# 128 more bytes ahead of the left-hand rooms of a decoder-layer kernel

## The chip, the cores and the metric

One core of one Trainium2 chip runs one launch of the kernel. The metric is the device time of that launch in microseconds (us), as the median of several runs. Lower is better.

## What is computed

One decoder layer over 1024 positions of width 1024, in float32 (each weight below is one layer's):

```python
h = rms_norm(x, ln_pre_mix)
proj = h @ w_in                      # pooling inputs (256), q, k, v (768 each)
q, k = rope(q, pos), rope(k, pos)    # 12 heads of 64
pool_out = multi_scale_pool(u_pool, w_pool, pool_scale)
attn_out = dilated_attention(q, k, v)        # three (window, dilation) settings, merged
mix = concatenate([pool_out, attn_out]) @ w_out
x = x + rms_norm(mix, ln_post_mix)
h = rms_norm(x, ln_pre_ffn)
f = (silu(h @ w_gate) * (h @ w_up)) @ w_down   # inner width 2816
x = x + rms_norm(f, ln_post_ffn)
```

## The kernel before

**Arithmetic.** Every large product is made in three passes: each operand is split into a high and a low half (ScalarE copies the high one, VectorE or GpSimd subtracts it for the low one), and TensorE adds up high x high, high x low and low x high (`PASSES`, line 167). So a product of one 128 x 128 weight block with 512 positions is three matmuls, each with its own weight load. In a matmul's name in the profile, `ps_o<-tT,fw 128*128 128x512` is: result in bank `o`, moving operand from a room `tT`, stationary operand (weights) from a room `fw`, 128 x 128 weights, 512 moving columns. A name that is in one place only, `ps_t<-fw`, has both operands in rooms of that name.

**Stages.** They follow one another on TensorE, with some overlap. To about 100 us: the first query and key projections (`first`, line 223), the value and pooling projections. To about 440 us: attention (`scores`, `merge`, `weigh`, `values`, lines 512 to 701) with projections of later heads filled in between (`proj_half`, line 412; `Fill`, line 389), so that runs of 512-column matmuls are cut into pieces of a few. To about 521 us: the output projection (`out_proj`, line 902), the norms (`chain`, line 1024) and the first gate and up blocks. To about 947 us: the gate and up products as seven block products in place of eight (`seven`, line 1178), 24 matmuls of 512 columns to a product, with the sums of weight blocks for the next stage beside them. To the end: the down projection, also in seven block products (`down`, line 1442), then the last norm and the stores.

**Order.** A list of steps with due times, written out by hand (`put`, `emit`, the numbers in `PRM`), sets the order of the matmuls; the matmuls are kept in program order (line 116). Loads and stores go out on SyncE's queue.

**Rooms.** SBUF is filled from two sides. On the left, from low addresses up, lie the pools `const`, `wpool`, `small`, and above them first `con1` and `att`, later, in the same place, `ffnl`. On the right, from high addresses down, lie `xg`, then `qkp`, later, in the same place, `mid`. The lines that matter:

```python
32   LEAD = {"const": 8, "con1": 8, "ffnl": 8}
...
121  const = ctx.enter_context(tc.tile_pool(name="const", bufs=1))
122  wpool = ctx.enter_context(tc.tile_pool(name="wpool", bufs=1))
...
169  half = const.tile([P, 1 + LEAD["const"]], F32, name="half")[:, :1]
...
188  xgp = ctx.enter_context(tc.tile_pool(name="xg", bufs=1, side="right"))
...
1061 r3 = ffnl.tile([P, T + LEAD["ffnl"]], F32, name="r3")[:, :T]
...
1273 for a, bb in PASSES:
1274     mm(banks[tag, i], lhs[:, i, a, c * P:(c + 1) * P], moving(b, bb, c),
```

`half` is the first tile of the first left-hand pool. It holds one number per partition, -0.5, the exponent of the reciprocal square root (line 184); `LEAD["const"]` adds eight numbers behind it that nothing reads. All later left-hand tiles start above it, at multiples of 32 bytes. A tile's start, in bytes of its partition and modulo 256, in the allocation of this kernel:

| side, pool | tiles, by their names in the profile | start modulo 256 |
|---|---|---|
| left, `wpool` | `whl` (split weights; operands of the block products), `wraw` | 0 |
| left, `att` | `pp`, `ptr`, `v`, `mix`, `dhl`, `wp`, `xraw` | 128 |
| left, `ffnl` | `b` (the normed features, split; later operands), `rw`, `op`, `q` | 0 |
| right, `qkp` | `k`, `qh`, `ql`, `vs` | 128 |
| right, `mid` | `fw` (operands; a feature block), `p`, `sq`, `rb` | 128 |
| right, `xg` | `x`, `m`, `z`, `tT` (sums of feature blocks), `op`, `xk`, `vlast`, `y` | 128 |

A block of weights within a room starts at a multiple of 512 bytes from the room's start, and a 512-column moving operand at a multiple of 1024, so each matmul's operands start at their room's place modulo 256. (The exceptions are matmuls of under 512 columns with strided keys.)

Of the kernel before, what the change touches and what calls it, by code (L numbers as in the profile page):

```python
# [28 lines left out]

LEAD = {"const": 8, "con1": 8, "ffnl": 8}

PRM = {'sqe': (0, 0, 0, 0, 1, 1, 0, 1),
        'sqa': (1, 0, 0, 1, 0, 0, 0, 1),
# [75 lines left out]
def hybrid_block(ctx: ExitStack, tc: tile.TileContext, xT, w_in, w_v, w_pin, w_pool, w_out, w_gate, w_up, w_down,  # L111
# [56 lines left out]

    half = const.tile([P, 1 + LEAD["const"]], F32, name="half")[:, :1]
    nc.vector.memset(half, -0.5)  # L170
# [26 lines left out]

    g1s = con1.tile([P, NK + LEAD["con1"]], F32, name="g1s")[:, :NK]
    nc.sync.dma_start(g1s, g1)
# [860 lines left out]
    ffnl = ctx.enter_context(tc.tile_pool(name="ffnl", bufs=1))  # L1060
    r3 = ffnl.tile([P, T + LEAD["ffnl"]], F32, name="r3")[:, :T]
    B = {}
# [504 lines left out]
```

## Time and profile before

| | us |
|---|---|
| median of 3 runs (1175.99 to 1178.06) | 1177.0 |
| the profiled execution's own time | 1176.04 |
| its span, first to last instruction | 1174.3 |
| TensorE busy (matmuls) | 1140.2 |
| VectorE / GpSimd / ScalarE busy | 792.1 / 602.0 / 543.3 |

The profile lists groups of equal instructions as `line engine operation out<-in shape xcount | busy us, mean ns of one`. Matmuls are pipelined: a mean of 390 ns is from one matmul's start to its end, and the next starts about 230 ns behind it. So the pace is read from starts, or from a group's busy time over its count, and not from the mean. PE is TensorE's matmul stream, PEld its weight loads, DVE VectorE, ACT ScalarE, POOL GpSimd, SP SyncE. A window row gives busy time and instructions per engine, then the granted TensorE clock, the share of the 16 DMA engines and GB/s.

### The profile page before, as it was taken

The page shows a single profiled execution, that of the slowest core. Times are in us where ns is not written, and L with a number is a line of the kernel's source. Part 1 is how long each engine was busy: PE and PEld are TensorE (multiplying, and loading weights), DVE is VectorE, ACT ScalarE, POOL GpSimd, SP SyncE. Part 2 cuts the span into 40 slices and gives each one's busy share as a digit, 9 for nine tenths or more (in the row PEclk, how much of TensorE's full clock was granted, in tenths as well). Part 3 has the DMA queues.
Part 4 walks back from the last instruction along what each step waited for, and adds up shares of the span by engine and source line. Part 5 has one row for each costly group of instructions (what it writes and reads, how often), then busy time and mean ns, then how long its engine had stood idle before and what let it go on. Part 6 is the DMA issues. An engine that isn't in the chain of part 4 may idle for free.

```text
span 1174.3 us, 17248 instructions
## 1 busy us (share of the span) xinstructions
PE 1140.2 (97%) x6134; PEld 980.7 (84%) x6134; DVE 792.1 (67%) x1477; ACT 543.3 (46%) x1033; POOL 602.0 (51%) x541
## 2 busy tenths in 40 slices
PE   8999999999998999999999999999999999999996
PEld 6998898999888888878888888888888888888896
DVE  7766878786887674869676655756465475454685
ACT  7356666666566574746432232223232435343430
POOL 0111646464565413250486656777665978566521
PEclk9999999999899999999999999999999999999998
DMA  7315151514124745722234545444535859666542
GB/s 269 99 62 180 37 180 37 180 55 162 54 83 157 264 166 187 275 73 99 75 141 143 192 158 187 181 164 160 204 127 187 284 196 376 229 203 190 191 143 72
DMA packets 85365, 188.51 MB, mean 161 GB/s; under 512 B 8736, under 2 KB 24352, under 8 KB 83872
## 3 DMA queue, kind: packets, MB, share of 16 engines
q1 hardware_dynamic: 84704, 186.90, 45.7%
q8 instruction: 48, 0.79, 0.3%
q10 hardware_dynamic: 576, 0.52, 0.1%
q14 instruction: 37, 0.30, 0.1%
HBM read 134.44 MB, written 52.95 MB: 160 GB/s over the span
## 4 chain that ended last, share of the span: by engine, by line
PE 82%; DVE 7%; ACT 4%; DMA 3%; issue 2%; POOL 2%; SPq 0%; ACTq 0%; POOLq 0%; DVEq 0%
PE ps_pj L116 28%; PE ps_o L116 22%; PE ps_s L116 21%; PE ps_t L116 9%; PE ps_t L119 2%; ACT pp L559 1%; DMA mixd<-mix 1%; DMA b<-in_w_out_dram 1%; DVE k L348 1%; DMA xraw<-in_xT_dram 1%; DVE whl L159 1%; DVE ptr L656 1%; DMA m<-mixd 1%; DVE sq L1005 0%; POOL whl L159 0%
## 5 line engine op out<-in xcount | busy, mean ns | idle before, releaser
L116 PE MATMUL ps_pj<-x,whl 128*128 128x512 f32 x480 | 145.4, 417 | 0.0
L1221 POOL TENSOR_TENSOR fw<-rw,fw 128x512 fp32r<-128x512 f32 x74 | 100.5, 1383 | 65.2 <-ACT fw L1219 65.2
L611 POOL TENSOR_SCALAR pp<-pp,wv 128x256 f32<-128x256 f32 (+1 forms) x156 | 72.0, 481 | 104.1 <-DVE wv L595 51.4
L116 PE MATMUL ps_o<-tT,fw 128*128 128x512 f32 x504 | 117.7, 389 | 0.0
L159 POOL TENSOR_TENSOR whl<-wraw,whl 128x512 fp32r<-128x512 f32 x50 | 66.7, 1355 | 90.9 <-ACT whl L155 61.0
L116 PEld LDWEIGHTS ps_o<-tT,fw 128*128 128x128 f32 x504 | 94.6, 188 | 19.9
L559 ACT ACTIVATE pp<-pp,sx 128x128 f32<-128x128 f32 (+1 forms) x192 | 89.3, 468 | 29.8 <-DVE sx L556 29.3
L116 PEld LDWEIGHTS ps_pj<-x,whl 128*128 128x128 f32 x480 | 87.0, 194 | 10.3 <-POOL whl L159 0.4
L1221 POOL TENSOR_TENSOR whl<-rw,whl 128x512 fp32r<-128x512 f32 x42 | 60.3, 1459 | 57.7 <-ACT whl L1219 57.7
L1219 ACT ACTIVATE fw<-rw 128x1024 fp32r<-128x1024 f32 x37 | 38.5, 1056 | 99.3 <-DVE rw L1187 34.3
L116 PE MATMUL ps_pj<-whl,x 128*128 128x256 f32 x528 | 80.6, 293 | 0.0
L1363 POOL TENSOR_TENSOR op<-rw,op 128x512 fp32r<-128x512 f32 x38 | 59.9, 1577 | 36.9 <-ACT op L1362 34.4
L656 DVE TENSOR_TENSOR ptr<-ps_t,ptr 128x512 fp32r<-128x512 f32 (+1 forms) x84 | 56.2, 669 | 25.0 <-ACT ptr L655 24.4
L116 PEld LDWEIGHTS ps_pj<-whl,x 128*128 128x128 f32 x528 | 70.8, 196 | 0.5 <-DVE whl L159 0.2
L1362 ACT ACTIVATE op<-rw 128x1024 fp32r<-128x1024 f32 x38 | 40.2, 1060 | 64.2 <-PE ps_t L116 27.0
L325 POOL TENSOR_TENSOR rsw<-rsw,sinr 128x512 f32<-128x512 f32 x20 | 26.2, 1310 | 84.5 <-DVE rsw L323 84.5
L655 ACT ACTIVATE ptr<-ps_t 128x512 fp32r<-128x512 f32 (+1 forms) x84 | 48.5, 577 | 40.9 <-PE ps_t L119 39.7
L116 PE MATMUL ps_o<-ptr,v 128*128 128x128 f32 (+1 forms) x472 | 58.8, 258 | 5.3 <-DVE ptr L656 5.3
L116 PE MATMUL ps_pj<-b,fw 128*128 128x512 f32 x264 | 63.3, 395 | 0.0
L116 PEld LDWEIGHTS ps_o<-ptr,v 128*128 128x128 f32 x472 | 52.4, 164 | 9.5 <-DVE ptr L656 6.4
L116 PEld LDWEIGHTS ps_pj<-b,fw 128*128 128x128 f32 x264 | 49.6, 188 | 11.9
L116 PE MATMUL ps_s<-k,qh 128*128 128x128 f32 (+1 forms) x192 | 53.6, 291 | 0.3 <-DVE sx L556 0.2
(302 smaller groups left out, 2917.2 us busy)
## 6 DMA issues: line engine op xcount, KB each, us to landing
rw<-bd SPq DMA_DIRECT2D x77, 256.0 KB, 4.9
v<-vd SPq DMA_DIRECT2D x22, 512.0 KB, 4.5
rw<-wsd SPq DMA_DIRECT2D x44, 256.0 KB, 4.0
rw<-in_w_gate_dram SPq DMA_DIRECT2D x20, 512.0 KB, 3.6
rw<-in_w_up_dram SPq DMA_DIRECT2D x20, 512.0 KB, 4.6
bd<-p SPq DMA_DIRECT2D x33, 256.0 KB, 2.5
rw<-in_w_down_dram SPq DMA_DIRECT2D x33, 256.0 KB, 4.6
fw<-in_w_down_dram SPq DMA_DIRECT2D x16, 512.0 KB, 4.0
```

The source lines that it names most:

```text
L116: return tc.keep_in_program_order(nc.tensor.matmul(*a, **k))
L119: return tc.keep_in_program_order(nc.tensor.transpose(dst, src, by))
L159: eng.tensor_tensor(dst[:, 1, at:at + w], src[:, at:at + w], dst[:, 0, at:at + w].bitcast(F32), ALU.subtract)
L325: eng[0].tensor_tensor(s, s, sinr[:, sl], ALU.mult)
L559: nc.scalar.activation(pt[:, j, lo:], pt[:, j, lo:], AF.Exp, bias=sx[:, 0, side, j, hd, 0:1], scale=-1.0, accum_out=sx[:, 0, side, j, hd, ...
L611: nc.gpsimd.tensor_scalar(pv, pv, un.wv[:, side, j, hd:hd + 1], 1.0, op0=ALU.mult, op1=ALU.mult)
L655: nc.scalar.activation(ptr[:, 0, :w], t[:, :w], AF.Copy)
L656: nc.vector.tensor_tensor(ptr[:, 1, :w], t[:, :w], ptr[:, 0, :w].bitcast(F32), ALU.subtract)
L1219: nc.scalar.activation(w[n][:, :, 0], raw[n], AF.Copy)
L1221: low[0] = nc.gpsimd.tensor_tensor(w[n][:, i, 1], raw[n][:, i], w[n][:, i, 0].bitcast(F32), ALU.subtract)
L1362: nc.scalar.activation(w[:, :, 0], raw, AF.Copy)
L1363: nc.gpsimd.tensor_tensor(w[:, 0, 1], raw[:, 0], w[:, 0, 0].bitcast(F32), ALU.subtract)
```

## The change

```diff
-LEAD = {"const": 8, "con1": 8, "ffnl": 8}
+LEAD = {"const": 40, "con1": 8, "ffnl": 8}
```

`half` grows from 36 to 164 bytes per partition. All left-hand tiles behind it move up by 128 bytes; the right-hand ones stay. Modulo 256, `wpool` and `ffnl` go from 0 to 128 and `att` from 128 to 0, while `qkp`, `mid` and `xg` stay at 128. Between the end of `att` and the start of `qkp` 256 bytes were free, so both still fit. No instruction is added, removed or moved; operands on the same side keep their distance.

## The prediction

> **What bounds the kernel now.** I read the busy times first, then the chain of waits, then the engines by stage, then the matmul groups by form in the stage that carries most.
>
> ```profile
> PE 1140.2 (97%) x6134; PEld 980.7 (84%) x6134; DVE 792.1 (67%) x1477; ACT 543.3 (46%) x1033; POOL 602.0 (51%) x541
> ...
> PE 82%; DVE 7%; ACT 4%; DMA 3%; issue 2%; POOL 2%; SPq 0%; ACTq 0%; POOLq 0%; DVEq 0%
> ```
>
> TensorE is busy nearly throughout and is 82% of the chain that ended last. The stages differ, though:
>
> ```profile
> 100.00:440.00 340.00, 325.21 (x2158) 297.47 (x2158) 266.02 (x779) 219.53 (x582) 166.98 (x215) 0.98 0.38 129
> 440.00:521.00 81.00, 78.00 (x391) 64.12 (x390) 51.85 (x64) 48.17 (x80) 27.89 (x25) 0.98 0.55 195
> 521.00:947.00 426.00, 425.91 (x1861) 348.08 (x1860) 271.38 (x323) 140.33 (x184) 272.24 (x199) 1.00 0.45 162
> 947.00:1174.30 227.30, 216.21 (x1096) 184.58 (x1094) 134.90 (x174) 83.43 (x91) 119.75 (x79) 0.98 0.59 200
> ```
>
> Columns: stretch, its length, busy time of PE, PEld, DVE, ACT, POOL, clock, DMA share, GB/s. From 521 to 947 us, the gate and up products, TensorE has no gap at all (425.91 of 426.00), at full clock; whatever a matmul costs there is paid in the end time, one for one. In attention (100 to 440) TensorE shares the path with others. So the question is whether the place of the operands changes what a matmul costs. In this stage the same matmul, 128 x 128 weights and 512 columns, is run from several combinations of rooms:
>
> ```profile
> L116 PE MATMUL ps_o<-tT,fw 128*128 128x512 f32 x504 | 117.7, 389 | 0.0
> L116 PE MATMUL ps_pj<-b,fw 128*128 128x512 f32 x264 | 63.3, 395 | 0.0
> L116 PE MATMUL ps_o<-tT,whl 128*128 128x512 f32 x216 | 52.0, 395 | 0.0
> L116 PE MATMUL ps_s<-b,fw 128*128 128x512 f32 x180 | 43.3, 395 | 0.0
> L116 PE MATMUL ps_pj<-b,whl 128*128 128x512 f32 x168 | 39.3, 390 | 0.0
> L116 PE MATMUL ps_s<-tT,fw 128*128 128x512 f32 x144 | 33.7, 389 | 0.0
> L116 PE MATMUL ps_s<-b,whl 128*128 128x512 f32 x129 | 30.4, 390 | 0.0
> L116 PE MATMUL ps_s<-tT,whl 128*128 128x512 f32 x96 | 23.0, 395 | 0.0
> L116 PE MATMUL ps_pj<-b,op 128*128 128x512 f32 x48 | 11.3, 395 | 0.0
> L116 PE MATMUL ps_t<-b,fw 128*128 128x512 f32 x36 | 8.7, 395 | 0.0
> L116 PE MATMUL ps_s<-fw,whl 128*128 128x512 f32 x12 | 3.0, 394 | 0.0
> L116 PE MATMUL ps_t<-fw,whl 128*128 128x512 f32 x12 | 2.9, 394 | 0.0
> ```
>
> The first name behind the arrow is the moving room, the second the weights. `tT`, `fw` and this `op` start at 128 modulo 256, `b` and `whl` at 0. Where both operands are at 128 (tT,fw) or both at 0 (b,whl) the mean is 389 or 390 ns; where one is at 0 and the other at 128 (all other rows) it is 394 or 395. The bank plays no part: `ps_o` and `ps_s` have both kinds. In order of time the difference is seen in the starts, 24 matmuls to a row:
>
> ```profile
> 638.00 5.61 PE L116 MATMUL ps_pj<-b,whl 128*128 128x512 f32 x24
> 643.44 5.61 PE L116 MATMUL ps_o<-tT,fw 128*128 128x512 f32 x24
> 648.89 5.75 PE L116 MATMUL ps_pj<-b,fw 128*128 128x512 f32 x24
> 654.48 5.62 PE L116 MATMUL ps_o<-tT,fw 128*128 128x512 f32 x24
> 659.94 5.75 PE L116 MATMUL ps_s<-tT,whl 128*128 128x512 f32 x24
> 665.52 5.74 PE L116 MATMUL ps_o<-tT,whl 128*128 128x512 f32 x24
> ```
>
> From start to start: b,whl 5.44 us, tT,fw 5.45, b,fw 5.59, tT,fw 5.46, tT,whl 5.58. An unequal product costs 0.14 us more than an equal one, 5.8 ns for each matmul.
>
> **The change part by part.** It does one thing: left-hand rooms go up by 128 bytes. Pairs with both operands on one side keep their distance. Pairs across the sides change: `whl`, `b` and `rw` go to 128, where `x`, `m`, `tT`, `fw` and `op` on the right already are, so the unequal rows above become equal; the attention rooms (`v`, `pp`, `ptr`) go from 128 to 0 and become unequal to `vlast` and to what streams from the right ahead of them.
>
> *Gate and up stage, 521 to 947 us.* The unequal rows above hold 264 + 216 + 180 + 96 + 48 + 36 + 12 + 12 = 864 matmuls, or 36 products of 24. At 0.14 us each that is 5.0 us, all on the path. Bounds: the shortest unequal product above against the longest equal one is 5.58 less 5.46, 0.12 us, or 4.3 us in all; by busy time over count, 63.3 / 264 = 239.8 ns for b,fw against 117.7 / 504 = 233.5 for tT,fw, 6.3 ns each, 5.4 us in all. Nothing waits to take the freed time: TensorE gains 1.2% here, and VectorE (271.38 us) and GpSimd (272.24), which make its operands, are busy for under two thirds of the stretch.
>
> On this the Trainium skill speaks against the change: TensorE: Matmul & The Clock Gate, Step-by-step: what each phase is for, says that "Loading the next tile's weights doesn't steal SBUF read bandwidth from the running matmul". By that rule the place of one against the other could not matter, and the sum would be nothing. This trace does not bear it out: 389 or 390 ns against 394 or 395, by nothing but the pair of rooms.
>
> *Output projection, 440 to 521 us.* Two rows show the same moving room with unequal and with equal weights:
>
> ```profile
> 461.16 5.04 PE L116 MATMUL ps_pj<-fw,whl 128*128 128x512 f32 x21
> ...
> 472.56 4.96 PE L116 MATMUL ps_pj<-fw,xk 128*128 128x512 f32 x21
> ```
>
> 0.08 us over 21 matmuls is 3.8 ns each, less than above: the runs are shorter and broken by other matmuls. In program order 208 unequal neighbours of 512 columns lie in this stretch, so 0.8 us, and TensorE is busy for 78.00 of 81.00 us: 0.7 us. Bounds: nothing (if the other engines set the pace), and 208 x 5.8 = 1.2 us.
>
> *To 440 us.* Some 470 unequal neighbours (first projections, fillers and output projection among attention) become equal. But here 512-column matmuls come in groups of three between others, and the rows with equal operands (`xk` is on the right, at 128) are no better off than those without:
>
> ```profile
> L116 PE MATMUL ps_pj<-m,whl 128*128 128x512 f32 x72 | 20.8, 408 | 0.8 <-DMA m<-mixd 0.8
> ...
> L116 PE MATMUL ps_pj<-m,xk 128*128 128x512 f32 x24 | 7.2, 404 | 0.0
> ```
>
> 20.8 / 72 is 289 ns and 7.2 / 24 is 300. I take 0.1 us, nearest to these rows; the bounds are nothing and 470 x 5.8 = 2.7 us. Products of 256 columns, the pooling and value projections, do not care either:
>
> ```profile
> L116 PE MATMUL ps_t<-whl,x 128*128 128x256 f32 x144 | 19.1, 283 | 0.0
> ...
> L116 PE MATMUL ps_t<-k,x 128*128 128x256 f32 x48 | 6.2, 284 | 0.0
> ```
>
> The first is unequal, the second equal: 283 and 284 ns. On the other side of the account, 174 neighbours go from equal to unequal: 76 matmuls of 512 columns from the right followed by a weight load from an attention room, and 98 of 128 or 256 columns, many of them around `vlast`. At the price of a 512-column pair that is 1.0 us at most; by the two rows above, nothing. I take nothing and keep 1.0 us for the range.
>
> *Last stage, 947 us to the end.* Each operand room there holds both operands of its products, so they are equal before and after. Only at the step from a room on one side to one on the other does the next weight load lie elsewhere: 43 neighbours, 0.2 us.
>
> *Vector engines and DMA.* Their operands move too, at no cost that I take: in the long stage VectorE and GpSimd have a third of the time free, and for loads these rows stand:
>
> ```profile
> fw<-in_w_down_dram SPq DMA_DIRECT2D x16, 512.0 KB, 4.0
> wsd<-fw SPq DMA_DIRECT2D x8, 1024.0 KB, 3.9
> ...
> whl<-in_w_down_dram SPq DMA_DIRECT2D x6, 512.0 KB, 4.0
> wsd<-whl SPq DMA_DIRECT2D x3, 1024.0 KB, 3.9
> ```
>
> `fw` is at 128, `whl` at 0: the same load lands after 4.0 us in both, the same store after 3.9.
>
> The sum is 5.0 + 0.7 + 0.1 + 0.2 = 6.0 us. The profiled execution took 1176.04 us (span 1174.3 and 1.7 around it), so a like one would take 1170.0. It lies 1.0 us below the median of the runs, 1177.0, so the median I forecast is 1171.0.
>
> **The rivals.** *It is the side, not the place modulo 256.* In the rows above, equal pairs are also pairs on one side of the memory, and unequal pairs are pairs across: `b` and `whl` are left, `tT`, `fw`, `op` right. The long matmuls of this trace never show a pair across the sides at one place, or a pair on one side at two. If what costs 5.8 ns is to read from two distant parts, the change does not do what it says, and the time stays at 1177.0. For it: nothing separates the two. Against it: two rooms in the same half would be expected to get in each other's way more, not less, if reads from one part compete, and the rows show the reverse. I give it 0.10. The Trainium skill's rule of the two reads that do not disturb each other (the page named above) would also give 1177.0.
>
> *Loads that start off a 256-byte boundary become the bound, and it is slower.* Place: the last stage, where every product needs its `rw` rooms loaded, which go from 0 to 128, and the DMA share is 0.59. Price: if packets into such rooms took twice as long, the transfers would need 2 x 0.59 = 1.18 of the 227.30 us; 41 us more, so 1212. It decides from a factor of 1 / 0.59 = 1.7. Against it stand the landing times above, a factor of 1.0. I give it 0.04. The Trainium skill, DMA: Bandwidth & Descriptors, How a descriptor splits into AXI transactions, says that a transfer not starting on a 256-byte boundary pays for an extra partial transaction; for a row of 2 KB I estimate from that page 68 beats in place of 64, 6% more, a share of 0.63, and no change in the end time. The two equal landings show nothing of it.
>
> *The attention stage gives it back.* The 174 neighbours made unequal, and a path there that runs through other engines, could take back some of the 6.0 us; to bring the gain under 2.4 us they would have to cost 3.6 us, over three times my bound. 0.02, at 1175.0.
>
> **How the numbers follow.** 0.84 is left for the forecast. The three runs span 2.07 us, 1.0 to either side, and 0.2% of 1177 (2.4 us) is about what a measurement can tell from no change. Low end: every bound at its most, 5.4 + 1.2 + 2.7 + 0.2 = 9.5 us, so 1167.5. High end: 4.3 us gained in the long stage alone, 1.0 given back by the pairs made unequal, 1.0 for the runs: 1177.0 - 4.3 + 1.0 + 1.0 = 1174.7. The range leaves out the side rival, the DMA rival and a little of the forecast's own case, 2 in 10 in all. Faster by over 0.2%: the forecast, 0.84. Within: the side rival and the attention rival, 0.10 + 0.02 = 0.12. Slower: the DMA rival, 0.04.
>
> **What would show it right or wrong.** In the changed kernel the rows b,fw, tT,whl, b,op and fw,whl should have a mean of 389 or 390 ns, and every product of 24 from 521 us on should take 5.44 or 5.45 us from start to start; the stretch now from 521 to 947 should be 5 us shorter, the last one equal within 0.3 us, the stretch to 440 us equal within 1. The landing of `rw` and `whl` loads should stay. Rows b,fw and tT,whl still at 395 would make the side rival right. Gaps on TensorE in the last stage, behind `rw` loads, would point to DMA.

## The result and the profile after

The changed kernel took 1169.93 us in the median of 6 runs (1167.2 to 1170.79), the kernel before 1176.42 us in 6 runs beside them: 6.5 us less, a ratio of 0.994 with a 95% interval of 0.9926 to 0.9954. The forecast was 1171.0 in 1167.5 to 1174.7. The profiled execution took 1170.79 us (span 1169.0), 5.25 us less than the profiled one before.

The page still shows TensorE as the bound; its busy time fell by 5.0 us, from 1140.2:

```profile
PE 1135.2 (97%) x6134; PEld 982.6 (84%) x6134; DVE 791.9 (68%) x1477; ACT 543.5 (46%) x1033; POOL 603.2 (52%) x541
...
PE 83%; DVE 6%; ACT 4%; DMA 3%; issue 2%; POOL 1%; SPq 0%; ACTq 0%; POOLq 0%; DVEq 0%
```

The same groups of matmuls in the same stage, by form:

```profile
L116 PE MATMUL ps_o<-tT,fw 128*128 128x512 f32 x504 | 117.5, 389 | 0.0
L116 PE MATMUL ps_pj<-b,fw 128*128 128x512 f32 x264 | 61.6, 389 | 0.0
L116 PE MATMUL ps_o<-tT,whl 128*128 128x512 f32 x216 | 50.7, 390 | 0.0
L116 PE MATMUL ps_s<-b,fw 128*128 128x512 f32 x180 | 42.2, 390 | 0.0
L116 PE MATMUL ps_pj<-b,whl 128*128 128x512 f32 x168 | 39.2, 389 | 0.0
```

All of these are now at 389 or 390 ns, and so are b,op and fw,whl, the other rows that were unequal. b,fw, across the sides, went from 63.3 to 61.6 us of busy time for the same 264 matmuls, 239.8 to 233.3 ns each; tT,fw and b,whl, equal before too, went from 117.7 to 117.5 us and from 39.3 to 39.2. In order of time:

```profile
637.18 5.60 PE L116 MATMUL ps_pj<-b,whl 128*128 128x512 f32 x24
642.62 5.60 PE L116 MATMUL ps_o<-tT,fw 128*128 128x512 f32 x24
648.06 5.60 PE L116 MATMUL ps_pj<-b,fw 128*128 128x512 f32 x24
653.50 5.60 PE L116 MATMUL ps_o<-tT,fw 128*128 128x512 f32 x24
658.94 5.60 PE L116 MATMUL ps_s<-tT,whl 128*128 128x512 f32 x24
664.38 5.60 PE L116 MATMUL ps_o<-tT,whl 128*128 128x512 f32 x24
```

From start to start every product takes 5.44 us, the unequal ones 0.14 or 0.15 less than before. The two last stretches, cut at the same matmuls as before:

```profile
521.71:942.04 420.33, 420.18 (x1861) 347.78 (x1860) 273.98 (x323) 140.00 (x182) 271.85 (x198) 1.00 0.45 164
942.04:1169.00 226.96, 215.91 (x1096) 184.52 (x1094) 132.68 (x175) 83.98 (x92) 120.37 (x80) 0.98 0.61 202
```

420.33 us in place of 426.00, still without a gap on TensorE; 226.96 in place of 227.30.

**Where the time went, stretch by stretch.** The order of the instructions is the same in all kernels here but one (the runs of matmuls alone), so a stretch can be cut at the same two matmuls in each trace. The table gives each stretch's length less that in the kernel before, in us. The marks are the matmuls that start at these times in the kernel before; the last column is the stretch from 947.03 to 1140.03.

```
                       16.06   33.03  100.05  440.17  521.01  550.06  947.03
                      -33.03 -100.05 -440.17 -521.01 -550.06 -947.03 -1140.03
before, length         16.97   67.02  340.12   80.83   29.05  396.97  193.01
the change             -0.37   +0.22   +0.29   +0.83   -0.61   -5.08   -0.37
the change, again      -0.33   +0.25   -0.29   -0.44   -0.35   -5.07   -0.37
ffnl alone             +0.01   -0.00   -0.56   +1.40   -0.04   -1.34   -0.21
all but ffnl           -0.38   +0.23   -2.29   +0.37   +0.06   -0.22   -0.13
256 bytes              -0.00   +0.00   -2.96   -0.01   +0.00   +0.05   -0.00
attention rooms back   -0.37   +0.22   -1.40   +0.72   -0.61   -5.10   -0.37
attention rooms alone  +0.05   +0.05   +1.45   +0.23   +0.00   -0.03   -0.00
64 bytes               -0.25   -0.70   -0.64   +0.91   +0.07   -0.03   +0.68
```

The two columns from 100 to 521 us are blurred by the clock: the kernel with 256 bytes, whose rooms all lie where they were modulo 256, is 2.96 us shorter there. The windows show why. First the kernel before, then the one with 256 bytes, over the same time (their traces agree to 0.02 us at the mark of 100 us):

```profile
305.25:312.07 6.82, 6.32 (x19) 5.29 (x20) 5.00 (x12) 1.86 (x4) 2.66 (x2) 0.50 0.26 78
```

```profile
305.25:312.07 6.82, 6.34 (x34) 5.42 (x35) 6.05 (x17) 2.41 (x5) 2.92 (x3) 1.00 0.26 78
```

In the first the granted clock was 0.50, and 19 matmuls were done where the other did 34 at 1.00. Such stretches of 3.4 or 6.8 us come between 100 and 521 us, where TensorE has gaps (and one of 9 to 13 us at the end of each trace). How many an execution gets changes from run to run: between 100 and 440 us the kernel before and the profiled change have 13.7 us of them, the change again 10.2, the kernel with 256 bytes 6.8. In these two columns one profile against another says nothing below some 3 us.

A part of attention is free of them: from 128 to 303 us all nine traces are at full clock. There the changed kernel differs from the one before by +0.02 us, again by -0.34, and all but ffnl, with the same places in this part, by -0.46; the two whose places are as before here differ by -0.22 (ffnl alone) and -0.09 (256 bytes). With the attention rooms back it is -0.72, with them alone +0.46. So what the change does here is a few tenths at most, hardly more than the difference between kernels with the same places.

### The profile page after: what moved, and what is told of

Read it like the earlier page. It is cut to its first block, busy times and chain, and to the rows that moved or that the text cites. A ratio compares the mean times of both kernels' runs of the same rounds, so it can differ in the third digit from the quotient of the medians.

```text
span 1169.0 us, 17248 instructions
## 1 busy us (share of the span) xinstructions
PE 1135.2 (97%) x6134; PEld 982.6 (84%) x6134; DVE 791.9 (68%) x1477; ACT 543.5 (46%) x1033; POOL 603.2 (52%) x541
## 4 chain that ended last, share of the span: by engine, by line
PE 83%; DVE 6%; ACT 4%; DMA 3%; issue 2%; POOL 1%; SPq 0%; ACTq 0%; POOLq 0%; DVEq 0%
PE ps_pj L116 28%; PE ps_o L116 22%; PE ps_s L116 21%; PE ps_t L116 9%; PE ps_t L119 2%; ACT pp L559 1%; DMA b<-in_w_out_dram 1%; DMA m<-mixd 1%; DMA mixd<-mix 1%; DVE k L348 1%; DMA xraw<-in_xT_dram 1%; DMA rw<-in_w_up_dram 0%; DVE ptr L656 0%; DVE whl L159 0%; DMA vd<-vs 0%
## 5 line engine op out<-in xcount | busy, mean ns | idle before, releaser
L116 PE MATMUL ps_o<-tT,fw 128*128 128x512 f32 x504 | 117.5, 389 | 0.0
L116 PEld LDWEIGHTS ps_pj<-x,whl 128*128 128x128 f32 x480 | 87.4, 194 | 10.2 <-POOL whl L159 0.4
L116 PE MATMUL ps_pj<-b,fw 128*128 128x512 f32 x264 | 61.6, 389 | 0.0
```

The costliest lines, as they stand in the source:

```text
L116: return tc.keep_in_program_order(nc.tensor.matmul(*a, **k))
```

## The experiments

The theory: what costs is that the operand that streams and the weights that are loaded meanwhile start at different places modulo 256 bytes. The main rival: what costs is that they lie on different sides of the memory. The experiments come first that separate the two.

**The ffnl rooms alone.** This puts `b` and `whl`, both on the left, at different places, and `b` and `fw`, on two sides, at one.

```diff
-LEAD = {"const": 8, "con1": 8, "ffnl": 8}
+LEAD = {"const": 8, "con1": 8, "ffnl": 40}
```

> The kernel before, with 128 bytes more ahead of the ffnl pool's rooms alone: b, rw and the left-hand op go to 128 modulo 256; whl stays at 0, the right-hand rooms at 128. Place theory (what counts is whether the streaming operand and the next weights start at the same place modulo 256): b,fw and b,op fall from 395 to 389 ns, b,whl rises from 390 to 395 although both are on the left, tT,whl stays at 395. Unequal neighbours between 521 and 947 us fall from 865 to 644, so 221 x 5.8 ns = 1.3 us less, about 1175.1. Side theory (what counts is whether both lie on one side): no row changes, b,whl stays at 390 and b,fw at 395, and the time stays at 1176.4.

Measured: 1174.07 us, a ratio of 0.9986 (0.9976 to 0.9996) to the kernel before. Its groups by form:

```profile
L116 PE MATMUL ps_o<-tT,fw 128*128 128x512 f32 x504 | 117.6, 389 | 0.0
L116 PE MATMUL ps_pj<-b,fw 128*128 128x512 f32 x264 | 61.7, 389 | 0.0
L116 PE MATMUL ps_o<-tT,whl 128*128 128x512 f32 x216 | 51.9, 395 | 0.0
L116 PE MATMUL ps_s<-b,fw 128*128 128x512 f32 x180 | 42.3, 390 | 0.0
L116 PE MATMUL ps_pj<-b,whl 128*128 128x512 f32 x168 | 40.2, 395 | 0.0
```

b,whl, fast before, is now at 395 though both rooms are on the left, and b,fw is at 389 across the sides. The stretch from 550 to 947 us lost 1.34 us, against the 221 x 5.8 ns = 1.3 us expected for 521 to 947 us. The side theory falls.

**Everything but the ffnl rooms.** The opposite half of the change.

```diff
-LEAD = {"const": 8, "con1": 8, "ffnl": 8}
+LEAD = {"const": 40, "con1": 8, "ffnl": 40}
```

> The changed kernel, with 128 bytes more ahead of the ffnl pool too, so that b, rw and the left-hand op are back at 0 modulo 256 and only whl (with the attention rooms) has moved. Place theory: tT,whl and fw,whl fall from 395 to 389 ns, b,whl rises from 390 to 395, b,fw stays at 395. Unequal neighbours: 837 between 521 and 947 us (865 before), 49 in the output projection (208 before), so about 0.2 + 0.6 us less than before, near 1175.5. Side theory: no row changes, 1176.4.

Measured: 1175.41 us, a ratio of 1.0002 (0.999 to 1.0013); the expected 0.8 us lies within the interval. Its rows:

```profile
L116 PE MATMUL ps_pj<-b,fw 128*128 128x512 f32 x264 | 63.4, 395 | 0.0
L116 PE MATMUL ps_o<-tT,whl 128*128 128x512 f32 x216 | 50.8, 390 | 0.0
...
L116 PE MATMUL ps_pj<-b,whl 128*128 128x512 f32 x168 | 40.3, 395 | 0.0
```

tT,whl is at 390, and both rows of `b` are at 395: again the place decides, not the side. Neither half of the change is worth much alone: what the one makes equal with the right-hand rooms it makes unequal with the other half.

**256 bytes in place of 128.**

```diff
-LEAD = {"const": 8, "con1": 8, "ffnl": 8}
+LEAD = {"const": 72, "con1": 8, "ffnl": 8}
```

> The kernel before with 256 bytes more ahead of all left-hand rooms in place of 128: every room is where it was modulo 256, but 256 bytes further up. Place theory with a period of 256 bytes: rows and time as before, b,fw and tT,whl at 395 ns, 1176.4. If it is the distance of the two sides itself, or any move, or a period of 512 bytes or more, that counts, rows change: 1170 if any move does it.

Measured: 1176.06 us, a ratio of 1.0005 (0.9993 to 1.0016), with b,fw and tT,whl at 395 and 550 to 947 us as before within 0.05. It is not the moving of the rooms that helps, and the period is 256 bytes or a part of it.

**The matmuls by themselves.** The kernel before, in one execution, with these runs behind its warm-up; `sc` is a right-hand room, `cross` a left-hand one at the same place modulo 256.

```diff
+    runs = [(sc, 512 + d // 4, (512,) * 48) for d in (0, 32, 64, 96, 128, 160, 192, 224, 256)]
+    runs += [(cross, d // 4, (512,) * 48) for d in (0, 128)]
+    runs += [(sc, 512 + d // 4, (256,) * 48) for d in (0, 128)]
+    runs += [(sc, 512 + d // 4, (512, 512, 512, 128, 128) * 16) for d in (0, 128)]
+    for n, (w, at, cols) in enumerate(runs):
+        tb = bank(("pj", "o")[n % 2])
+        for c in cols:
+            mm(tb[:, :c], w[:, at:at + P], sc[:, :c], start=True, stop=True)
```

> The kernel before, with matmuls of zeros added behind the ten warm-up matmuls; their results are not used, and the added time is no part of the layer. Fifteen runs on two banks in turn: nine of 48 matmuls of 512 columns with the weights in the same room as the streaming operand and 0, 32, 64, 96, 128, 160, 192, 224 and 256 bytes off its place modulo 256; two with the streaming operand on the right and the weights in a left-hand room, 0 and 128 bytes off; two of 256 columns, 0 and 128 off, in one room; two broken ones, three of 512 columns and two of 128 in turn, 16 times, 0 and 128 off. Place theory: 0 and 256 settle at 5.44 us for 24, so 10.9 us for 48; 128 takes 11.2; the two across the sides are as those within one room, 10.9 and 11.2; 256 columns show no difference; the broken pair differs by less than 48 x 5.8 ns = 0.28 us if equal streams have to settle first. Side theory: the nine within one room all take 10.9 us, the two across both take 11.2.

The timeline has one row for each of the fifteen runs, in the order of the code: start, length to the last end, count. A run's cost is the next row's start less its own.

```profile
5.93 11.69 PE L116 MATMUL ps_pj<-sc 128*128 128x512 f32 x48
17.46 11.35 PE L116 MATMUL ps_o<-sc 128*128 128x512 f32 x48
28.65 11.36 PE L116 MATMUL ps_pj<-sc 128*128 128x512 f32 x48
39.85 11.40 PE L116 MATMUL ps_o<-sc 128*128 128x512 f32 x48
51.09 11.32 PE L116 MATMUL ps_pj<-sc 128*128 128x512 f32 x48
62.25 11.37 PE L116 MATMUL ps_o<-sc 128*128 128x512 f32 x48
73.45 11.16 PE L116 MATMUL ps_pj<-sc 128*128 128x512 f32 x48
84.45 11.36 PE L116 MATMUL ps_o<-sc 128*128 128x512 f32 x48
95.64 11.04 PE L116 MATMUL ps_pj<-sc 128*128 128x512 f32 x48
106.52 11.05 PE L116 MATMUL ps_o<-sc,cr 128*128 128x512 f32 x48
117.41 11.32 PE L116 MATMUL ps_pj<-sc,cr 128*128 128x512 f32 x48
128.56 5.91 PE L116 MATMUL ps_o<-sc 128*128 128x256 f32 x48
134.31 5.85 PE L116 MATMUL ps_pj<-sc 128*128 128x256 f32 x48
140.00 14.73 PE L116 MATMUL ps_o<-sc 128*128 128x512 f32 x80
154.56 14.79 PE L116 MATMUL ps_pj<-sc 128*128 128x512 f32 x80
```

The first run, 0 bytes off, still begins at the slow clock of the start (its first three starts are 427, 427 and 426 ns apart); its twin, 256 off, takes 106.52 - 95.64 = 10.88 us, 226.7 ns for each matmul. 32, 64, 96, 128, 160 and 224 bytes off take 11.16 to 11.24, some 233 ns; 192 off takes 11.00. Across the sides 0 off takes 10.89 and 128 off 11.15: the side does nothing. Nor does it take another engine:

```profile
62.25:95.64 33.39, 33.39 (x145) 27.02 (x144) 0.00 (x0) 0.00 (x0) 0.00 (x0) 1.00 0.00 0
95.64:117.41 21.77, 21.77 (x98) 18.02 (x96) 0.00 (x0) 0.00 (x0) 0.00 (x0) 1.00 0.00 1
```

From 62 to 117 us VectorE, ScalarE and GpSimd do nothing and the DMA share is 0.00, and still the run 224 off takes 11.19 us there and the two equal ones 10.88 and 10.89. Only the place of the weights was varied here, and in the kernel equal rows stand both at 0 and at 128, so what counts is the distance between TensorE's own two operands; that their reads meet is the likely reading and was not seen directly.

Three more things stand in the trace under these rows. In the first run, behind these three, the starts are 249, 236, 228, 232 and 231 ns apart and only then 227: an equal stream can take some matmuls to settle. It need not: the run 256 off, behind an unequal one, has 226 or 227 from its first matmul on. In the broken runs nothing is left of the gain. From the first start to the start behind the last they take 14.57 us equal and 14.62 unequal, but 49 ns of these 56 lie in the first group of five alone (866 against 915 ns), which has another run ahead of it. Behind it every group takes 913 or 914 ns equal, and 911 to 922, in the mean 913.8, unequal. And at 256 columns the equal run is the slower one, 134.31 - 128.56 = 5.75 us against 5.69, some 1.1 ns for each.

**The changed kernel again, and with the attention rooms back at 128.** The second is the version in which no large room lies apart.

```diff
-LEAD = {"const": 40, "con1": 8, "ffnl": 8}
+LEAD = {"const": 40, "con1": 40, "ffnl": 8}
```

> The changed kernel once more, beside the next ones on the same chip. Place theory, with its sizes: 5 us less between 521 and 947 us, 0.4 to 0.5 less by 100 us, 0.2 to 0.3 less behind 947; in all 1169 to 1170.5 against 1176.

> The changed kernel with 128 bytes more ahead of con1 and att as well: the attention rooms are back at 128 modulo 256, where all large rooms of both sides now are; no 512-column pair is unequal, and none of the 174 smaller or mixed pairs that the change made unequal is left so. Place theory: at most 174 x 5.8 ns = 1.0 us less than the changed kernel; if pairs of under 512 columns and broken runs do not care, as the runs of matmuls alone show, the same time within 0.2 us. If the attention stage gave something back, this run takes it: over 1.0 us less.

Measured on one chip beside 1176.38 for the kernel before: 1169.74 for the changed kernel, a ratio of 0.9949 (0.9936 to 0.9962), and 1169.22 with the attention rooms back, 0.9944 (0.9931 to 0.9957). The intervals overlap; 0.5 us between the medians is within the bound of 1.0, and cannot be told from nothing.

**The attention rooms alone.**

```diff
-LEAD = {"const": 8, "con1": 8, "ffnl": 8}
+LEAD = {"const": 8, "con1": 40, "ffnl": 8}
```

> The kernel before, with 128 bytes more ahead of con1 and att alone: the attention rooms go to 0 modulo 256, wpool and ffnl stay at 0, the right-hand rooms at 128. The part of the change that could cost, by itself: the 174 pairs become unequal, nothing becomes equal. Place theory: as before or up to 1.0 us slower; 521 to 947 us unchanged. If attention rooms at another place than vlast and the streams ahead of them cost more, it is slower by over 1.0 us.

Measured: 1176.0 us, a ratio of 0.9996 (0.9986 to 1.0006). That the change moves these rooms away from the right-hand ones costs nothing that the times can show.

**64 bytes in place of 128.**

```diff
-LEAD = {"const": 8, "con1": 8, "ffnl": 8}
+LEAD = {"const": 24, "con1": 8, "ffnl": 8}
```

> The kernel before with 64 bytes more ahead of all left-hand rooms in place of 128: the two sides are 64 or 192 bytes apart modulo 256 instead of 128. By the matmuls alone (0 off: 226.7 ns, 64 off: 233.4, 128 off: 232.5, 192 off: 228.9) b,fw and b,op, whose weights lie 64 behind the stream, cost as much as before or 1 ns more, and tT,whl and fw,whl, 192 behind, some 3 ns less; 336 pairs of the one and 529 of the other kind, whichever way the difference is counted, make at most 529 x 3.6 = 1.9 us less, 1174 to 1176. If half the distance were half the way to the changed kernel, it would be 1173.

Measured: 1175.42 us, a ratio of 0.9994 (0.9985 to 1.0003); 550 to 947 us as before within 0.03. In this stretch half the way is no part of the gain. The small advantage of 192 off, which the run of matmuls alone had, hardly showed there: this kernel's rows

```profile
L116 PE MATMUL ps_pj<-b,fw 128*128 128x512 f32 x264 | 63.4, 394 | 0.0
L116 PE MATMUL ps_o<-tT,whl 128*128 128x512 f32 x216 | 51.7, 395 | 0.0
```

have tT,whl at 51.7 / 216 = 239.4 ns, 1.3 less than before and not 3.6. Why it is less is open. Elsewhere 64 bytes did act, and the starts in the trace say where. From 16 to 33 us x,whl, 192 off, saved 0.25 us, two thirds of what equal rooms save. From 33 to 100 us the 262 matmuls of 256 columns with `whl` streaming and the weights from `x`, 64 off, came 118.5 ns apart in place of 121.2, which is the 0.70 us. In the last stretch, behind some of the steps from one room to another, it took up to ten starts of 224 to 236 ns to come back to 227, which is the 0.68 us.

## Why the prediction was right

**The gate and up stage** (forecast 5.0 us, bounds 4.3 and 5.4). From 550 to 947 us the change saved 5.08, 5.07 and 5.10 us in three profiles in which all rooms of this stage are equal. The first part, 521 to 550, gave another 0.35 to 0.61, so 5.4 to 5.7 in all. The mechanism was right, and the size a little low: 761 of the 865 unequal neighbours lie behind 550, so 5.08 us is 6.7 ns for each and not 5.8. Within the products, tT,whl and b,fw went from 233.3 ns to 227.0 or 227.1. With all rooms equal every product takes 5.44 us, also the equal ones that took 5.45 or 5.46 behind an unequal one. Nothing took the freed time.

**The output projection** (forecast 0.7). The saving in the matmuls is there: the 236 matmuls of 512 columns from 440 to 521 us whose next start follows within 260 ns in all nine traces take 54.69 us before and 53.85, 53.85 and 53.87 in the three profiles, 0.8 us less. Whether it reaches the end is not settled: the stretch differs by +0.83, -0.44 and +0.72. The clock differs, and part of the saving goes into a longer wait. Before and in the changed kernel again, which both have 3.4 us of halved clock there, TensorE's wait in this stretch is

```profile
PE ps_o L116 <- DVE sq L1005: 2.9, 2, 2.1
```

```profile
PE ps_o L116 <- DVE sq L1005: 3.6, 2, 2.7
```

So the forecast had the matmuls right and took too little account of the norm that follows on VectorE (its sum of squares, line 1005).

**To 440 us** (forecast 0.1). From 16 to 33 us the first projections saved 0.33 to 0.38 in all four kernels in which `whl` was level with `x`, and nothing (+0.01, -0.00, +0.05) in the three in which it was 128 off. There the 512-column matmuls come in one unbroken run of 70, which I had lumped with attention; 69 pairs at 5.8 ns make 0.40. Behind them, from 33 to 100 us, the same four kernels lost 0.22 to 0.25. That is the part of the prediction that failed: "Products of 256 columns, the pooling and value projections, do not care either". They care the other way. By themselves they cost 1.1 ns more when equal. In place, from start to start, the 262 matmuls with `whl` streaming, the weights from `x` and another of their kind behind take 121.1 to 121.4 ns in the four kernels in which the two are 128 off and 122.1 in each of the four in which they are equal, 0.2 us in all; those with `k` streaming, whose places did not change, stay at 121.4 to 121.7 in all nine. The mean of a group, 283 against 284 ns, was too coarse to show it. So up to 100 us the forecast of 0.1 came out by luck: 0.1 us net, from a gain of 0.37 and a loss of 0.22 that it had both at next to nothing.

In attention the reading held that broken runs gain little. Of the x,whl matmuls from 100 to 440 us, 208 have another of their kind behind, full clock, and under 260 ns to the next start in all nine traces. They take 232.2 to 232.7 ns in the four kernels with `whl` 128 off and 230.4 to 231.0 in the four with it level: 2 ns in place of 5.8, 0.4 us in all. The 256-column matmuls show no loss here (from 128 to 303 us 125.7 to 126.4 ns unequal, 126.0 to 126.2 equal). On the other side, the 1008 other matmuls of attention that are free of the halved clock and under 140 ns in all traces take 94.99, 94.99 and 95.00 us with the places of the changed kernel, 94.75 to 94.85 with those of before and 94.74 with the attention rooms back, so some 0.2 us are given back; with the attention rooms alone it is 94.82, and which pairs cost it was not separated.

**The last stage** (forecast 0.2). 0.37 us by the mark of 1140, in three profiles. The 43 neighbours were the right ones, but a step between rooms also unsettles the matmul behind it: at the one from `fw` to `op` at 960.4 us the starts before are 233 and 231 ns apart, in the changed kernel 226 and 227. So a step costs 0.37 / 43 = 8.6 ns and not 5.8.

**The sum.** The columns that the clock does not disturb give -0.37 + 0.22 - 0.61 - 5.08 - 0.37 = -6.2 us for the profiled change, and -5.9 for its second profile. The medians say 6.5 and 6.6. The two profiled executions differ by 5.25, mostly because the changed one has 3.4 us more of halved clock between 440 and 521 us. A fraction of a microsecond to 16 us and between 100 and 521 us stays unassigned. That 6.0 came so near 6.5 is in part luck: the long stage and the last one gave some 0.6 to 0.9 us more than forecast, and the output projection's 0.7 cannot be found in the end time. Of the 1.1 us between the forecast median and the measured one, 0.6 is that the kernel before ran at 1176.42 and not at 1177.0.

**The rivals.** The side fell with the ffnl rooms alone, and with the two runs across the sides. The Trainium skill says that loading the next weights does not take read bandwidth from the running matmul (TensorE: Matmul & The Clock Gate, Step-by-step: what each phase is for). The runs of matmuls alone do not bear that out, with 226.7 ns against some 233 by the place of the weights only. The DMA rival fell with the landing times. Before:

```profile
rw<-bd SPq DMA_DIRECT2D x77, 256.0 KB, 4.9
...
rw<-wsd SPq DMA_DIRECT2D x44, 256.0 KB, 4.0
...
rw<-in_w_down_dram SPq DMA_DIRECT2D x33, 256.0 KB, 4.6
```

And in the changed kernel:

```profile
rw<-bd SPq DMA_DIRECT2D x77, 256.0 KB, 4.9
...
rw<-wsd SPq DMA_DIRECT2D x44, 256.0 KB, 4.0
...
rw<-in_w_down_dram SPq DMA_DIRECT2D x33, 256.0 KB, 4.8
fw<-in_w_down_dram SPq DMA_DIRECT2D x16, 512.0 KB, 4.1
```

`rw` went from 0 to 128 modulo 256 and lands as before (4.6 became 4.8 in the third row, as it did with 256 bytes, where `rw` stayed at 0); `fw`, which did not move, went from 4.0 to 4.1. TensorE waits for no load in the last stage, before or after. Attention as the one that gives it back fell with the attention rooms alone and back: what it takes is some tenths, not 3.6 us.

## What to carry to other kernels

Where TensorE is the bound and every matmul loads new weights, compare the groups of one shape by the rooms that they read: a constant few nanoseconds between them, by start to start, can be a layout cost that a few bytes of padding take away. Count the pairs that the padding makes unequal as well as those that it makes equal, and only in long runs of such matmuls; here one half of the change alone was worth a quarter of it, the other nothing. Cut both traces at the same matmuls, and look at the granted clock of each stretch before believing a difference.

## What the runs showed of the hardware

With 512 columns in float32r, streams whose operand and next weights start at the same place modulo 256 bytes settle at 226.7 ns a matmul, at once or after up to eight matmuls (behind a break, at 521.71 us of the changed kernel, the starts are 315, 230, 236, 228, 233 and 231 ns apart, then 226). 32, 64, 96, 128, 160 or 224 bytes apart they stay at some 233, and 192 apart at 229 by themselves. It is not a matter of degree: 64 bytes nearer gained nothing in the long stage. At 256 columns the order is reversed, 119.7 ns equal and 118.6 ns 128 bytes apart. What in the memory does this was not measured.
